# A sixth tile pair of an up projection formed from seven products, and what stands behind it in the order

## The chip, the core and the metric

The kernel runs on one core of one Trainium2 chip. The metric is the device time of one execution in microseconds (us). Five engines work side by side and meet only through semaphores: PE (matmuls), DVE and ACT (elementwise work), POOL (here mostly DMAs that add) and SP (plain DMAs). Each runs its own list of instructions in the order in which the program holds them.

## The reference

One layer of a decoder over 512 prompt rows and 8 sequences of 4 sample rows, 544 rows in all. The change lies in its last part, the convolutional feed-forward block:

```python
def _conv_ffn(h, prev, w_up, conv_w, conv_b, w_down):
    u = h @ w_up                                   # 1024 -> 8192
    u, conv_state = _causal_dwconv(u, prev, conv_w, conv_b)
    val, gate = jnp.split(u, 2, axis=-1)
    return (jax.nn.gelu(gate, approximate=True) * val) @ w_down, conv_state   # 4096 -> 1024
```

All matrix products are made in float32 accuracy from pairs of rounded high and low parts.

## The kernel before, in words

Each factor is split into a high part H and a low part L, and a product of blocks is the sum high times high, high times low, low times high: three matmuls for each of the 128-row pieces of the contraction. The up projection is made in 32 pairs p: column tile p of the value half and column tile 32+p of the gate half, 128 columns each. The normed rows lie in two halves of 272 (`b11`, `b21` for rows 0 to 271, upper and lower half of the contraction; `b12`, `b22` for rows 272 to 543).

A pair is made in one of two ways. The plain way takes eight half products of 12 matmuls each (two tiles, two halves of the contraction, two row halves; bank names `pq`). The other, from pair `PLAIN` on, forms seven products of 12 matmuls from sums of weights and sums of rows (function `pair`; banks `pux`, `puy`, `puz` and sometimes `puw`): `a11`, `a12`, `p2`, `p3`, `p1`, `p4`, `a22`. The rows' sums `t1` to `t4` are made once, ahead of the first such pair. The weights' sums are made per pair by `sums`: DVE forms p3 = s + g and g = g + g', and two adding DMAs of POOL form the rest in place, in a third loaded weight tile (`raw_up_..._s`). Banks are read in between: `e1` is bank x after `a11`, and `p2` adds onto that bank only when the copy is taken; `u4` is bank x after `p1`; from it DVE forms the gate's second row half out of bank y (`u` from `puy` and `u4`), and only then may `a22` add onto bank y.

After a pair come, per tile, the state copies, a convolution of three taps (`tap`: ACT, then DVE twice, into `uc`), and `glu`: a gelu on ACT, the product `z` on DVE, its high part `fH` on ACT and its low part `fL` on DVE. These feed the down projection, made per group of four pairs (quarter products `dn`, q = 0 to 6: one output tile c, one row half a, 12 matmuls, banks `pmdn`); the last group (pairs 28 to 31, weights `dl`) comes at the end with products of its own.

Every weight tile is rounded on ACT (`wh_...`, line 1485) and its remainder taken on DVE (`wl_...`). The order of the work is a list, `plan`, written ahead. After each step of the list (a product), the elementwise work that is due and the splits of the weights some steps ahead are put down; so each engine's order follows from the place of the products in the list. Half products of the down projection are put in behind certain products of a pair (`places`), as far as the group that they need is `ready`, which is counted in steps of the list:

```python
            places = [x for x in todo_ if x[2] in LAST_PLACES.get(p_, ("a12", "p3", "p1", "a22"))]
...
            ready[p_] = len(plan) + CHAIN + 3
```

What is left of them at the end of the list stands behind the last pair, except three that are held back. A pair whose `p1` is followed at once by another product of a pair is `apart`: its `p4` goes to a bank of its own (`puw`), and DVE, in place of ACT, forms the tile's second row half from it.

Of the kernel before, what the change touches and what calls it, by code (L numbers as in the profile page):

```python
# [11 lines left out]
F32 = mybir.dt.float32  # L12
# [5 lines left out]
P = 128  # L18
# [42 lines left out]
YA = (0.5, 0.5)  # L61
YB = (0.5, 0.5)
EARLY = 4
PLAIN = 6
FB = (1.0,)
LASTS = 6
HELD = 5
# [56 lines left out]
def hawk_step(ctx, tc, I, O):  # L124
# [18 lines left out]
    def S(name, dt=F32):  # L143
        return sp.tile([P, SLOT], dt, tag="s", name=name)
# [28 lines left out]
    def add(out, a, b):  # L173
        dve.tensor_tensor(out=out, in0=a, in1=b, op=ALU.add)  # L174
# [1033 lines left out]
    def part_pool(which):  # L1208

        if not parts:  # L1210
            trans.close()
            parts["e"] = ctx.enter_context(tc.tile_pool(name="parts", bufs=E_BUFS))
            parts["p"] = ctx.enter_context(tc.tile_pool(name="psums", bufs=2))
        return parts[which]
# [171 lines left out]
    for p_ in range(EARLY, 32):  # L1386
        if p_ < PLAIN:
            todo_ = [("q", j, u, a) for j in (p_, 32 + p_) for u in range(2) for a in range(2)]
# [20 lines left out]
    raws, usplit, used = {}, {}, [0, 0, 0]  # L1409
# [41 lines left out]
    def source(key):  # L1451
        if key[0] in "eq":
            return raws["up", key[1], ""][:, 4 * key[2]:4 * key[2] + 4, :]
        if key[0] == "dn":
            return raws[key]
        if key[0] == "dl":
            return raws[key[:2]][:, 4 * key[2]:4 * key[2] + 4, :]
        _, p_, nm = key
        if nm == "p3":
            return raws["p3", p_]  # L1460
        r = raws["up", 32 + p_ if nm in ("p1", "a22") else p_, "s" if nm in ("p2", "p4") else ""]
        if isinstance(r, list):
            return r[nm == "p4"]
        return r[:, 0:4, :] if nm in ("a11", "p1", "p2") else r[:, 4:8, :]

    def sums(p_, part):
        w = {nm: source(("s", p_, nm)) for nm in ("p1", "p2", "p4", "a22")}
        if part == 0:
            raws["p3", p_] = part_pool("p").tile([P, 4, P], F32, tag="p", name=f"p3_{p_}")
            add(raws["p3", p_], w["p2"], w["p1"])  # L1470
        else:
            add(w["p1"], w["p1"], w["a22"])
            pool.dma_start(out=w["p2"], in_=w["p1"], accum_op=ALU.add)
            pool.dma_start(out=w["p4"], in_=w["p2"], accum_op=ALU.add)  # L1474
# [21 lines left out]
    def ahead(n, lag=1):  # L1496

        def upto_(z, m, f):
            while used[z] < min(m, len(units)):
                f(units[used[z]])  # L1500
                used[z] += 1
        upto_(0, n + LOADS, lambda key: [load(r) for r in needs(key)])
        while used[2] < min(n, len(units)):
            m = used[2] + 1
            upto_(2, m, do_high)
            upto_(1, m - lag, do_low)
        upto_(1, n - lag, do_low)
        while sumq and sumq[0][0] <= n + 1:
            sums(*sumq.pop(0)[1:])
# [498 lines left out]
```

## Time and profile before

| | us |
|---|---|
| median of 3 runs (977.48 to 978.67) | 977.74 |
| the profiled execution's own time | 977.74 |
| its span | 976.0 |
| PE busy | 967.6 |
| DVE busy | 758.6 |
| ACT busy | 551.0 |
| POOL busy | 168.8 |

The span is the stretch from the first to the last instruction of the profile; 1.74 us lie around it. The share of busy time is a mean over stages: the feed-forward block runs from about 419 us to the end.

### The profile page before, as it was taken

The page shows a single profiled execution, that of the slowest core. Times are in us where ns is not written, and L with a number is a line of the kernel's source. Part 1 is how long each engine was busy: PE and PEld are TensorE (multiplying, and loading weights), DVE is VectorE, ACT ScalarE, POOL GpSimd, SP SyncE. Part 2 cuts the span into 40 slices and gives each one's busy share as a digit, 9 for nine tenths or more (in the row PEclk, how much of TensorE's full clock was granted, in tenths as well). Part 3 has the DMA queues.
Part 4 walks back from the last instruction along what each step waited for, and adds up shares of the span by engine and source line. Part 5 has one row for each costly group of instructions (what it writes and reads, how often), then busy time and mean ns, then how long its engine had stood idle before and what let it go on. Part 6 is the DMA issues. An engine that isn't in the chain of part 4 may idle for free.

```text
span 976.0 us, 20122 instructions
## 1 busy us (share of the span) xinstructions
PE 967.6 (99%) x7668; PEld 959.9 (98%) x7668; DVE 758.6 (78%) x1632; ACT 551.0 (56%) x1344; POOL 168.8 (17%) x288
## 2 busy tenths in 40 slices
PE   9999999999999999999999999999999999999997
PEld 8999999999999999999999999999999999999996
DVE  5777888857858555699967888787888888888875
ACT  6544443467476435556767665655555555556652
POOL 2152000003306331230011111101011101011024
PEclk9999999999999999999999999999999999999999
DMA  7875535632334547136157585858586766768612
GB/s 217 237 239 163 151 88 147 161 93 87 109 113 126 175 121 189 45 122 184 39 114 189 126 191 129 184 137 177 140 179 157 169 156 160 166 140 221 201 30 92
DMA packets 234204, 143.07 MB, mean 147 GB/s; under 512 B 25012, under 2 KB 218940, under 8 KB 234076
## 3 DMA queue, kind: packets, MB, share of 16 engines
q1 hardware_dynamic: 224300, 120.21, 43.9%
q0 software_dynamic: 9696, 19.42, 11.9%
q10 hardware_dynamic: 112, 2.17, 0.6%
q8 instruction: 60, 0.98, 0.4%
q14 instruction: 36, 0.29, 0.1%
HBM read 115.59 MB, written 15.17 MB: 134 GB/s over the span
## 4 chain that ended last, share of the span: by engine, by line
PE 97%; DVE 1%; ACT 1%; DMA 0%; issue 0%; SPq 0%; POOL 0%; ACTq 0%; POOLq 0%
PE pmin L165 20%; PE pmdn L165 19%; PE pux L1536 16%; PE puy L1536 8%; PE pq L1536 7%; PE pmout L165 5%; PE pmlo L165 5%; PE pmao L165 5%; PE puz L1536 4%; PE pg L165 1%; PE pvp L165 1%; PE psc L165 1%; PE ptok L165 1%; DMA pt<-pd 0%; PE ps_warm L165 0%; PE pm_first L165 0%
## 5 line engine op out<-in xcount | busy, mean ns | idle before, releaser
L165 PE MATMUL pmin<-hH,wh_in 128*128 128x256 f32 (+1 forms) x568 | 164.0, 291 | 0.0
L165 PE MATMUL pmin<-hL,wh_in 128*128 128x256 f32 (+1 forms) x568 | 162.5, 288 | 0.0
L165 PE MATMUL pmin<-hH,wl_in 128*128 128x256 f32 (+1 forms) x568 | 159.3, 288 | 0.0
L165 PE MATMUL pmdn<-fH,wh_dn 128*128 128x256 f32 (+1 forms) x448 | 129.3, 289 | 0.0
L165 PE MATMUL pmdn<-fH,wl_dn 128*128 128x256 f32 (+1 forms) x448 | 129.2, 288 | 0.0
L165 PE MATMUL pmdn<-fL,wh_dn 128*128 128x256 f32 (+1 forms) x448 | 129.0, 288 | 0.0
L165 PEld LDWEIGHTS pmin<-hH,wh_in 128*128 128x128 f32 x568 | 107.3, 189 | 1.2 <-issue 1.0
L165 PEld LDWEIGHTS pmin<-hL,wh_in 128*128 128x128 f32 x568 | 107.4, 189 | 0.1
L165 PEld LDWEIGHTS pmin<-hH,wl_in 128*128 128x128 f32 x568 | 104.8, 188 | 0.2 <-issue 0.2
L177 DVE SCALAR_TENSOR_TENSOR uc<-u,fv,uc 128x560 f32<-128x560 f32 x128 | 102.0, 797 | 1.7 <-ACT uc L1567 1.1
L165 PEld LDWEIGHTS pmdn<-fL,wh_dn 128*128 128x128 f32 x448 | 84.4, 188 | 0.0
L165 PEld LDWEIGHTS pmdn<-fH,wl_dn 128*128 128x128 f32 x448 | 84.4, 188 | 0.0
L165 PEld LDWEIGHTS pmdn<-fH,wh_dn 128*128 128x128 f32 x448 | 84.4, 188 | 0.0
L1664 ACT COPY u<-pux 128x272 f32<-128x272 f32 x52 | 20.1, 386 | 84.4 <-PE pux L1536 84.2
L168 DVE TENSOR_TENSOR u<-puy,u 128x240 f32<-128x240 f32 (+2 forms) x78 | 24.6, 343 | 48.8 <-PE puy L1536 32.2
L174 DVE TENSOR_TENSOR ft<-ft,pmdn 128x256 f32<-128x256 f32 (+1 forms) x104 | 45.0, 434 | 15.7 <-PE pmdn L165 15.7
L283 ACT ACTIVATE wh_in<-raw_in 128x512 fp32r<-128x512 f32 x70 | 42.2, 625 | 20.7 <-issue 11.0
L290 DVE TENSOR_TENSOR wl_in<-raw_in,wh_in 128x512 fp32r<-128x512 f32 x70 | 47.8, 694 | 1.0 <-ACT wh_in L283 1.0
L1567 ACT ACTIVATE uc<-u,fv 128x560 f32<-128x560 f32 x64 | 48.2, 755 | 0.0
L779 ACT ACTIVATE s<-s,st 128x256 f32<-128x256 f32 (+1 forms) x32 | 15.2, 475 | 53.8 <-DVE st L776 46.1
L168 DVE TENSOR_TENSOR wl_dn<-raw_dn,wh_dn 128x512 fp32r<-128x512 f32 x56 | 38.3, 685 | 3.8 <-ACT wh_dn L1485 3.8
L1474 POOL DMA_DIRECT2D raw_up_s<-raw_up_s x26 | 22.4, 861 | 95.8 <-DMA raw_up_s<-raw_up__11277 5.4
(761 smaller groups left out, 3388.5 us busy)
## 6 DMA issues: line engine op xcount, KB each, us to landing
raw_in<-in_w_in_dram SPq DMA_DIRECT2D x35, 512.0 KB
raw_dn<-in_w_down_dram SPq DMA_DIRECT2D x56, 256.0 KB
raw_up_s<-in_w_up_dram SPq DMA_DIRECT2D x25, 512.0 KB
raw_up_s<-raw_up_s POOLq DMA_DIRECT2D x26, 256.0 KB, 5.3
raw_ao<-in_w_attn_o_dram SPq DMA_DIRECT2D x8, 512.0 KB
raw_lo<-in_w_lru_o_dram SPq DMA_DIRECT2D x8, 512.0 KB
raw_out<-in_w_out_dram SPq DMA_DIRECT2D x8, 512.0 KB
pd<-pb SPq DMA_DIRECT2D x12, 256.0 KB
```

The costliest lines, as they stand in the source:

```text
L165: pe.matmul(out, l, r, start=start, stop=stop)
L168: dve.tensor_tensor(out=out, in0=a, in1=b, op=ALU.subtract)
L174: dve.tensor_tensor(out=out, in0=a, in1=b, op=ALU.add)
L177: dve.scalar_tensor_tensor(out=out, in0=a, scalar=s_, in1=b, op0=op0, op1=op1)
L283: act.activation(hl[0], raw, AF.Copy)
L290: (eng or dve).tensor_tensor(out=hl[1], in0=raw, in1=f32(hl[0]), op=ALU.subtract)
L779: act.activation(s3[:, j, :], s3[:, j, :], AF.Exp, bias=ng[:, j:j + 1], accum_out=sm[:, j:j + 1])
L1474: pool.dma_start(out=w["p4"], in_=w["p2"], accum_op=ALU.add)
L1536: pe.matmul(ps[:, :HN], w, x, start=start and k == 0 and i == 0, stop=stop and k == 3 and i == 2, skip_group_check=True)
L1567: act.activation(yt[j][:, 0:FLATU], u[:, 0:FLATU], AF.Copy, scale=fv[:, j:j + 1])
L1664: act.copy(e[nm_], z)
```

## The change

The constant `PLAIN` goes from 6 to 5, so pair 5, the sixth, is formed from seven products instead of eight. Its p3 lies in a slot of the general ring of 53 slots, in place of a tile of the small pool for such sums, which cannot be opened as long as the tiles of the norm before it are in use.

```diff
-PLAIN = 6
+PLAIN = 5
...
         if part == 0:
-            raws["p3", p_] = part_pool("p").tile([P, 4, P], F32, tag="p", name=f"p3_{p_}")
+            if p_ == PLAIN:
+                raws["p3", p_] = S(f"p3_{p_}")[:, 0:512].rearrange("p (k n) -> p k n", k=4)
+            else:
+                raws["p3", p_] = part_pool("p").tile([P, 4, P], F32, tag="p", name=f"p3_{p_}")
             add(raws["p3", p_], w["p2"], w["p1"])
```

With one step less in pair 5, readiness counted in steps comes at other places in each pair. Worked out from the list's code: before, no pair is `apart`; now pairs 8, 12, 16, 20, 24 and 28 are, where the down products of the next group, not yet ready, leave the place between `p1` and `p4` empty (and stand in a row a few steps later). Behind the last pair's `p4` stood five half products of the down projection, (6,4,0), (6,4,1), (6,5,1), (6,6,1) and (6,7,1); now the first two of them stand ahead of `p4`, and three are left. At the start of pair 5 no down product stands between `a12` and `p2`.

The order on DVE at pair 12, from the low part of its `p1` weights to the subtraction that frees bank y (`u44` from `puy_12`), before (in the names, the last number is the buffer's):

```order
L168 TENSOR_TENSOR wl_s_12_p1_8558<-raw_up_44__8255,wh_s_12_p1_8557 128x512
L174 TENSOR_TENSOR p3_13_8596<-raw_up_13_s_8489,raw_up_45__8487 128x512
L168 TENSOR_TENSOR wl_dn_1_7_8593<-raw_dn_1_7_8323,wh_dn_1_7_8592 128x512
L174 TENSOR_TENSOR raw_up_45__8487<-raw_up_45__8487 128x512
L177 SCALAR_TENSOR_TENSOR z11_8634<-uc11_8512,fv_264,uc43_8533 128x512
L177 SCALAR_TENSOR_TENSOR z11_8634<-uc11_8512,fv_264,uc43_8533 128x32
L168 TENSOR_TENSOR wl_s_12_p4_8615<-raw_up_12_s_8257,wh_s_12_p4_8614 128x512
L174 TENSOR_TENSOR ft6_7660<-ft6_7660,pmdn_1_6_1_8621 128x288
L168 TENSOR_TENSOR wl_s_12_a22_8640<-raw_up_44__8255,wh_s_12_a22_8639 128x512
L1543 MEMSET u44_8675 128x2
L168 TENSOR_TENSOR u44_8675<-puy_12_8598,u4_12_8673 128x240
L168 TENSOR_TENSOR u44_8675<-puy_12_8598,u4_12_8673 128x8x4
```

And the same place after:

```order
L168 TENSOR_TENSOR wl_s_12_p1_8607<-raw_up_44__8302,wh_s_12_p1_8606 128x512
L168 TENSOR_TENSOR wl_s_12_p4_8645<-raw_up_12_s_8304,wh_s_12_p4_8644 128x512
L177 SCALAR_TENSOR_TENSOR z11_8681<-uc11_8559,fv_264,uc43_8580 128x512
L177 SCALAR_TENSOR_TENSOR z11_8681<-uc11_8559,fv_264,uc43_8580 128x32
L168 TENSOR_TENSOR wl_s_12_a22_8665<-raw_up_44__8302,wh_s_12_a22_8664 128x512
L174 TENSOR_TENSOR ft7_7712<-ft7_7712,pmdn_1_7_1_8668 128x288
L168 TENSOR_TENSOR wl_s_13_a11_8687<-raw_up_13__8427,wh_s_13_a11_8686 128x512
L1546 MEMSET u44_8722 128x2
L168 TENSOR_TENSOR u44_8722<-puy_12_8648,u4_12_8720 128x240
L168 TENSOR_TENSOR u44_8722<-puy_12_8648,u4_12_8720 128x8x4
```

The first low part of the next pair's weights now stands ahead of the subtraction, and between `p1` and `a22` PE has one product instead of two.

The order on DVE at the end, from the second and third tap of tile 63 (`uc63`, the gate tile of pair 31) to the low part of the last pair's result (`fL31`), before:

```order
L177 SCALAR_TENSOR_TENSOR uc63_13070<-u63_13025,fv_264,uc63_13070 128x560
L168 TENSOR_TENSOR wl_dn_6_6_13074<-raw_dn_6_6_12812,wh_dn_6_6_13073 128x512
L168 TENSOR_TENSOR wl_dn_6_7_13093<-raw_dn_6_7_12854,wh_dn_6_7_13092 128x512
L174 TENSOR_TENSOR ft4_7426<-ft4_7426,pmdn_6_4_0_13113 128x256
L177 SCALAR_TENSOR_TENSOR uc31_13131<-u31_12965,fv_264,uc31_13131 128x560 x2
L177 SCALAR_TENSOR_TENSOR z31_13149<-uc31_13131,fv_264,uc63_13070 128x512
L177 SCALAR_TENSOR_TENSOR z31_13149<-uc31_13131,fv_264,uc63_13070 128x32
L168 TENSOR_TENSOR wl_dl_0_0_13153<-raw_dl_0_12877,wh_dl_0_0_13152 128x512
L168 TENSOR_TENSOR wl_dl_1_0_13156<-raw_dl_1_12902,wh_dl_1_0_13155 128x512
L174 TENSOR_TENSOR ft4_7426<-ft4_7426,pmdn_6_4_1_13133 128x288
L168 TENSOR_TENSOR fL31_13178<-z31_13149,fH31_13177 128x544
```

The same stretch on DVE after, from the second low part of the last group's weights on (ahead of it stand `wl_dn_6_6`, `wl_dn_6_7`, the addition to `ft4`, the last tap of `uc63` and `wl_dl_0_0`):

```order
L168 TENSOR_TENSOR wl_dl_1_0_13163<-raw_dl_1_12929,wh_dl_1_0_13162 128x512
L168 TENSOR_TENSOR wl_dl_2_0_13168<-raw_dl_2_12954,wh_dl_2_0_13167 128x512
L168 TENSOR_TENSOR wl_dl_3_0_13192<-raw_dl_3_12977,wh_dl_3_0_13191 128x512
L174 TENSOR_TENSOR ft5_7471<-ft5_7471,pmdn_6_5_1_13171 128x288
L177 SCALAR_TENSOR_TENSOR uc31_13189<-u31_13015,fv_264,uc31_13189 128x560 x2
L177 SCALAR_TENSOR_TENSOR z31_13214<-uc31_13189,fv_264,uc63_13136 128x512
L177 SCALAR_TENSOR_TENSOR z31_13214<-uc31_13189,fv_264,uc63_13136 128x32
L168 TENSOR_TENSOR wl_dl_0_1_13195<-raw_dl_0_12906,wh_dl_0_1_13194 128x512
L168 TENSOR_TENSOR wl_dl_1_1_13218<-raw_dl_1_12929,wh_dl_1_1_13217 128x512
L1756 STREAM_TRANSPOSE ffn_rows_s3_13225<-sfT_5298 128x256
L174 TENSOR_TENSOR ft6_7581<-ft6_7581,pmdn_6_6_1_13198 128x288
L168 TENSOR_TENSOR fL31_13242<-z31_13214,fH31_13241 128x544
```

Four low parts of the last group's weights now stand ahead of the taps of `uc31`, where none stood, and two more and a transposition between `z31` and `fL31`.

The order on ACT over the same stretch, from the gelu of tile 63 to the last tile's high part `fH31`, before (`u31` from `pux_31` is the copy of the last product `p4`):

```order
L1578 ACTIVATE uc63_13070<-uc63_13070,fv_264 128x560
L1485 ACTIVATE wh_dn_6_7_13092<-raw_dn_6_7_12854 128x512
L1681 COPY u31_12965<-pux_31_12908 128x240
L1681 COPY u31_12965<-pux_31_12908 128x8x4
L1559 COPY u31_12965<-sfT_5298 128x8x2
L1560 COPY sfT_5298<-u31_12965 128x16
L1561 COPY stage_p_5299<-u31_12965 128x2
L1567 ACTIVATE uc31_13131<-u31_12965,fv_264 128x560
L1485 ACTIVATE wh_dl_0_0_13152<-raw_dl_0_12877 128x512
L1485 ACTIVATE wh_dl_1_0_13155<-raw_dl_1_12902 128x512
L1485 ACTIVATE wh_dl_2_0_13159<-raw_dl_2_12925 128x512
L1586 ACTIVATE fH31_13177<-z31_13149 128x544
```

And after (the row ahead of these is again the gelu of tile 63, the row behind them one more split, and then `fH31`):

```order
L1488 ACTIVATE wh_dl_1_0_13162<-raw_dl_1_12929 128x512
L1488 ACTIVATE wh_dl_2_0_13167<-raw_dl_2_12954 128x512
L1684 COPY u31_13015<-pux_31_12960 128x240
L1684 COPY u31_13015<-pux_31_12960 128x8x4
L1562 COPY u31_13015<-sfT_5298 128x8x2
L1563 COPY sfT_5298<-u31_13015 128x16
L1564 COPY stage_p_5299<-u31_13015 128x2
L1570 ACTIVATE uc31_13189<-u31_13015,fv_264 128x560
L1488 ACTIVATE wh_dl_3_0_13191<-raw_dl_3_12977 128x512
L1488 ACTIVATE wh_dl_0_1_13194<-raw_dl_0_12906 128x512
L1488 ACTIVATE wh_dl_1_1_13217<-raw_dl_1_12929 128x512
```

Two splits instead of one stand between the gelu and the copies of `p4`, and the split `wh_dl_3_0`, for which `wl_dl_3_0` on DVE waits, stands behind the first tap of `uc31`.

## The prediction

> **What bounds the kernel now.** I read the page first (busy time by engine, then the shares of the chain that ended last), then PE's waits, then the stages that the change touches.
>
> ```profile
> span 976.0 us, 20122 instructions
> PE 967.6 (99%) x7668; PEld 959.9 (98%) x7668; DVE 758.6 (78%) x1632; ACT 551.0 (56%) x1344; POOL 168.8 (17%) x288
> PE 97%; DVE 1%; ACT 1%; DMA 0%; issue 0%; SPq 0%; POOL 0%; ACTq 0%; POOLq 0%
> ```
>
> PE is busy 99% of the span and carries 97% of the chain. The list of what PE waited for (us in total, times, longest) has three entries, two of which are:
>
> ```profile
> PE pst L909 <- DVE ss L787: 0.7, 1, 0.7
> PE pm_first L165 <- DVE wh_in L285: 0.6, 1, 0.6
> ```
>
> None lies in the feed-forward block. So the time is PE's work, every product removed counts in full, and every new wait of PE is added in full. The question is only whether removing a product makes waits where there were none. Durations below come from the profiled execution, whose own time is the median of the runs, 977.74; 1.74 of it lie around the span and are taken as unchanged.
>
> **The saved product.** The chain of waits around pair 8 (start, duration, engine, tile, instructions):
>
> ```profile
> 542.72 1.50 PE pux L1536 x12
> 544.22 1.41 PE pmdn L165 x12
> 545.63 1.51 PE pux L1536 x12
> 547.14 1.51 PE puy L1536 x12
> ```
>
> These are `p1`, a half product of the down projection, `p4` and `a22`. A product costs 1.51. Pair 5 needs seven, not eight: **-1.5**. That is 0.15% of the time; a measurement of this kernel can tell some 0.2% (2.0 us) from no change. So with no new wait the change would not be seen at all, and the waits decide.
>
> **The tail.** The chain of waits at the end of the last pair:
>
> ```profile
> 921.91 1.60 PE pmdn L165 x12
> 923.51 1.52 PE pux L1536 x12
> 925.03 8.88 PE pmdn L165 x68
> 933.91 0.04 issue
> 933.95 1.00 PE pmdn L165 x4
> ```
>
> The last `p4` ends at 925.03. Five half products (1.60 each, the row of 921.91) fill PE until 933.0, and of the next product nine matmuls come before the last tile's rows are read. What must be made meanwhile stands on ACT and DVE; first ACT's timeline (start, duration, line, out<-in, idle before):
>
> ```profile
> 925.74 0.77 ACT L1578 ACTIVATE uc<-uc,fv 128x560 f32<-128x560 f32 x1 [2.03 <-DVE uc L177]
> 926.41 0.62 ACT L1485 ACTIVATE wh_dn<-raw_dn 128x512 fp32r<-128x512 f32 x1
> 926.93 0.42 ACT L1681 COPY u<-pux 128x240 f32<-128x240 f32 x2
> ...
> 927.70 0.76 ACT L1567 ACTIVATE uc<-u,fv 128x560 f32<-128x560 f32 x1
> 928.37 1.66 ACT L1485 ACTIVATE wh_dl<-raw_dl 128x512 fp32r<-128x512 f32 x3
> 931.12 0.66 ACT L1586 ACTIVATE fH<-z 128x544 fp32r<-128x544 f32 x1 [1.09 <-DVE z L177]
> ```
>
> And DVE's:
>
> ```profile
> 923.94 0.69 DVE L168 TENSOR_TENSOR wl_dn<-raw_dn,wh_dn 128x512 fp32r<-128x512 f32 x1
> 924.55 0.45 DVE L174 TENSOR_TENSOR ft<-ft,pmdn 128x288 f32<-128x288 f32 x1
> 924.91 0.80 DVE L177 SCALAR_TENSOR_TENSOR uc<-u,fv,uc 128x560 f32<-128x560 f32 x1
> ...
> 928.49 1.64 DVE L177 SCALAR_TENSOR_TENSOR uc<-u,fv,uc 128x560 f32<-128x560 f32 x2 [0.41 <-ACT uc L1567]
> 930.17 0.91 DVE L177 SCALAR_TENSOR_TENSOR z<-uc,fv,uc 128x512 f32<-128x512 f32 x2
> 931.00 1.29 DVE L168 TENSOR_TENSOR wl_dl<-raw_dl,wh_dl 128x512 fp32r<-128x512 f32 x2
> ...
> 932.57 0.72 DVE L168 TENSOR_TENSOR fL<-z,fH 128x544 fp32r<-128x544 f32 x1
> ...
> 935.98 0.44 DVE L1753 STREAM_TRANSPOSE ffn_rows_s<-sfT 128x256 f32<-128x256 f32 x1
> ```
>
> The reader is to see the chain `p4` copy 926.93, first tap 927.70, two taps to 930.17, `z` to 931.00, `fH` to 931.78, `fL` to 933.29, while PE reads these rows at about 934.2 (933.0 and nine matmuls, a ninth of 1.60 over twelve each being 0.13). So the cover is about 1 us. Around 933.9 PE lost something to other work: four matmuls of 0.13 took 1.00 with the issue gap 0.04, where 0.53 is their due; of the 0.5 between, some 0.2 may be the last matmul's length, so I take 0.3 as lost.
>
> After, three half products stand behind `p4`, so with `p4` again ending at 925.03 PE is at 925.03 + 3 x 1.60 + 1.20 = 931.03 when it asks for `fH31`. The chain, on the other hand, gets longer, by steps read off the rows. A low part costs DVE 0.61 (923.94 to 924.55), an addition 0.36 (924.55 to 924.91), a high part costs ACT 0.52 (926.41 to 926.93).
>
> - One more low part ahead of the last tap of `uc63`: +0.61. One more high part on ACT behind the gelu: +0.52. The copies of `p4` come at 926.93 + 1.13 = 928.06, the first tap 0.77 later, at 928.83, and ends at 929.59.
> - `wl_dl_3_0` on DVE needs `wh_dl_3_0`, which ACT makes right behind that tap: 928.83 + 0.67 + 0.62 = 930.12. Then 0.61 for the low part and 0.36 for the addition to `ft5`: the taps of `uc31` begin at 931.09, not at 928.49. What is queued behind the waiting low part is the whole rest of the chain.
> - Taps 1.68, so `z` at 932.77 and `fH31` 0.95 later, from 933.72 to 934.38. PE waits 934.38 - 931.03 = 3.35.
> - DVE is through with `z` at 933.60; two low parts (1.22), the transposition (0.36 to the next start) and an addition (0.36) stand ahead of `fL31`, which then ends at 935.54 + 0.72 = 936.26. PE has two matmuls (0.27) between `fH31` and this: it waits 936.26 - 934.38 - 0.27 = 1.61.
>
> Together 4.96, less the 0.3 already lost: **+4.7**. Bounds: if nothing on the chain got longer, 933.29 against 931.03 + 0.27, less 0.3, leaves +1.7; if `wh_dl_3_0` came behind two further high parts, +4.7 + 1.04 = +5.7. I take the chain as worked out, since each step is an order fixed on in-order engines.
>
> **The six pairs with `p4` right behind `p1`.** The timelines of the three engines in pair 8:
>
> ```profile
> 546.97 0.29 PE L1536 MATMUL puy<-t4H,wh_s_a 128*128 128x272 f32 x1
> ```
>
> ```profile
> 544.25 0.39 ACT L1664 COPY u<-pux 128x272 f32<-128x272 f32 x1 [0.57 <-PE pux L1536]
> ```
>
> ```profile
> 544.67 0.51 DVE L168 TENSOR_TENSOR u<-puy,u 128x240 f32<-128x240 f32 x2 [1.44 <-ACT u L1664]
> ```
>
> `u4` is copied as soon as `p1` ends, DVE subtracts until 545.18, and `a22` asks for bank y at 546.97: 1.79 of cover. Without the half product between (1.41) the cover is 0.38. A low part (0.61) that stands ahead of the subtraction uses it up and costs 0.23; one more high part on ACT (0.62) ahead of the copy makes it 0.85; two low parts and an addition on DVE give 0.61 + 0.61 + 0.45 - 0.38 = 1.29. Nothing lost is the lower end, 6 x 1.29 = 7.7 the upper. The order after has one low part ahead in pair 12, and DVE was idle 1.44 before the subtraction in pair 8, so I go near the one-instruction price, 0.4 a pair: **+2.4**. The half product itself isn't lost: it stands elsewhere in the list.
>
> **The start of pair 5.** `p2` adds onto bank x only when ACT has copied `e1`. In the order after, the copy stands behind the high parts of the row sums `t4H`, the copy of `u36`'s first rows, a split, its other copies with the states, and one more split; and no down product stands between `a12` and `p2`. In the timeline of ACT these were:
>
> ```profile
> 481.67 1.19 ACT L1308 ACTIVATE t4H<-h2f 128x544 fp32r<-128x544 f32 x2
> 482.76 0.36 ACT L1627 COPY u<-pq 128x272 f32<-128x272 f32 x1
> 483.02 0.63 ACT L1485 ACTIVATE wh_dn<-raw_dn 128x512 fp32r<-128x512 f32 x1
> ```
>
> 1.19 + 0.36 + 0.63 + 0.77 (copies and states, 926.93 to 927.70) + 0.62 + the copy 0.39 = 3.96. If ACT begins this when pair 4 ends, it is through 3.96 - 2 x 1.51 = 0.94 after `a12`: **+0.9**. If all of it is still there when `a11` ends, 2.45; if ACT was ahead, 0. I take the middle case.
>
> **What is costed at nothing.** Pair 5 now has seven splits, not four (3 x 0.61 more on DVE, 3 x 0.62 on ACT), two sums on DVE (0.61 each, taken as a low part of the same size) and two adding DMAs with a third loaded tile. The stretches around it (length, then PE, PEld, DVE, ACT, POOL busy) and the DMA's issue to landing:
>
> ```profile
> 480.00:490.00 10.00, 10.00 (x82) 10.00 (x81) 9.71 (x18) 6.94 (x18) 0.94 (x1) 1.00 0.41 114
> 490.00:500.00 10.00, 10.00 (x82) 10.00 (x81) 5.50 (x10) 6.01 (x21) 0.87 (x1) 1.00 0.62 150
> ```
>
> ```profile
> raw_up_s<-raw_up_s POOLq DMA_DIRECT2D x26, 256.0 KB, 5.3
> ```
>
> DVE's 3.05 fit into the 4.5 idle of the second stretch, not into the 0.29 of the first; without that cover 1.5 to 3 would show in pair 5's products. PE waited for no such DMA; if one came a whole landing late, 5.3. SP's loads shift by one tile, with the DMA engines at 0.41 to 0.62. I take 0 for all of it.
>
> **Sum:** -1.5 + 4.7 + 2.4 + 0.9 = +6.5, so 977.7 + 6.5 = **984.2 us**.
>
> **A rule on the clock.** At PE's start, in its timeline:
>
> ```profile
> 1.00 2.50 PE L165 MATMUL ps_warm<-ones 128*128 128x128 f32 x10 [1.00 <-POOL ones L219]
> ...
> 6.69 0.39 PE L165 MATMUL ps_warm<-ones 128*128 128x128 f32 x2
> ```
>
> The same matmul takes 0.25 in the first row and 0.20 in the second: a slow start of some 5.7 us, and between then and the tail no wait of PE is above 0.7. The Trainium skill, page "TensorE: Matmul & The Clock Gate", Part 1, section "What's actually happening", has PE fall to half its clock after an idle window of about 3.4 us and come back after as long a busy one; no run here shows PE idle for so long. By that page, as an estimate, the tail's wait would cost 1.7 more (half of 3.4), 985.9 in all; without it the sum stands.
>
> **Rivals.**
> 1. The tail alone: the six pairs and pair 5's start are hidden. -1.5 + 4.7 = +3.2: 981.0. For it speaks the idle DVE before the subtraction (1.44); against it a cover of only 0.38.
> 2. The six pairs pay in full: -1.5 + 4.7 + 7.7 + 0.9 = +11.8: 989.5. For it speaks a DVE busy 78% on the mean; against it the same idle.
> 3. PE slows after the tail's wait of 3.35 (at half rate for as long as the slow start, 5.7, half of it lost): +6.5 + 2.9 = +9.4: 987.1. The rows of the start speak for a clock that has to be earned, the small ratio of 0.25 to 0.20 against the full price.
> 4. Not slower: DVE and ACT run ahead, so that the four low parts in the tail are done while they would idle (2.03 on ACT before the gelu, 0.41 on DVE before the taps). Then the tail costs its lower bound and the rest is hidden: -1.5 + 1.7 = +0.2, 977.9. It decides where all new waits together stay under 3.5. Against it: `wl_dl_3_0` cannot start ahead of `wh_dl_3_0`, which stands behind the first tap.
> 5. No new wait at all: 977.7 - 1.5 = 976.2. Against it: 925.03 + 4.8 lies ahead of even the old `fH31`.
>
> **How the numbers follow.** The forecast, with its terms somewhat off (+4.5 to +8.5), has 0.53; rival 1 0.18, 2 0.07, 3 0.09, 4 0.08, 5 0.05. The time is that of the likeliest, 984.2. The range runs from 980.3 (the tail alone, its term 0.7 smaller) to 988.0 (the clock's loss, with a margin of 0.9): it leaves out rivals 2, 4 and 5, 0.20. Faster by over 0.2% needs 975.8 or less: 0.02, the lower edge of rival 5. Same: the rest of 5 and rival 4 and the lowest edge of rival 1, 0.13. Slower: 0.85.
>
> **What would show it.** PE's list of waits should have entries where it had none: the down products of the last group waiting for `fH31` (about 3.4) and `fL31` (about 1.6), `a22` of pairs 8 to 28 in steps of four for DVE's subtraction (0.2 to 0.9 each), and `p2` of pair 5 for ACT's copy (about 0.9). PE's busy time should fall by 1.5. If the wait for `fH31` is under 1, the tail's step is wrong; if PE waits for the adding DMAs of pair 5, what I costed at nothing is; if matmuls behind the tail's wait take longer than 0.13, the clock is.

## The result and the profile after

| | before | after |
|---|---|---|
| median, us | 977.74 | 987.54 (985.97 to 988.15, 5 runs) |
| ratio to before | | 1.0096 (95% interval 1.0085 to 1.0108) |
| the profiled execution's own time | 977.74 | 986.73 |
| its span | 976.0 | 984.9 |

The changed kernel is slower by 9.8 us in the median and 9.0 in the profiled execution, which is the one taken apart below. The page of the changed kernel, its first lines and the shares of the chain that ended last:

```profile
span 984.9 us, 20143 instructions
PE 968.4 (98%) x7656; PEld 960.0 (97%) x7656; DVE 765.8 (78%) x1653; ACT 551.5 (56%) x1334; POOL 169.2 (17%) x290
PE 87%; DVE 6%; ACT 3%; DMA 2%; issue 1%; SPq 0%; DVEq 0%; ACTq 0%
```

Twelve matmuls are gone, yet PE's busy time rose by 0.8 where 1.5 less was due: some of the others got slower. And DVE and ACT now carry a share of the chain (followed back from a wait, the chain runs over other engines for longer than PE stood still, so its shares are not losses). The list of PE's waits (us in total, times, longest), as far as they lie in the feed-forward block:

```profile
PE pmdn L165 <- ACT fH L1589: 3.4, 1, 3.4
PE pmdn L165 <- DVE fL L168: 1.4, 1, 1.4
PE puy L1539 <- DVE u L168: 1.3, 2, 1.1
...
PE pux L1539 <- ACT e L1667: 1.0, 1, 1.0
```

All four are where the prediction had put them. At the kernel's start two waits differ as well (`pm_first` 1.1, not 0.6, and a new one of 0.5 on the DMA of the input rows), but the matmuls behind them start at 9.20, and at 9.22 before: they cost nothing. The chain that makes the last tile's rows, on ACT and on DVE (the timelines; the product behind the last `p4` starts at 929.35, at 925.03 before):

```profile
932.55 0.42 ACT L1684 COPY u<-pux 128x240 f32<-128x240 f32 x2
...
933.31 0.76 ACT L1570 ACTIVATE uc<-u,fv 128x560 f32<-128x560 f32 x1
933.98 2.17 ACT L1488 ACTIVATE wh_dl<-raw_dl 128x512 fp32r<-128x512 f32 x4
938.22 0.66 ACT L1589 ACTIVATE fH<-z 128x544 fp32r<-128x544 f32 x1 [2.06 <-DVE z L177]
```

```profile
934.62 0.69 DVE L168 TENSOR_TENSOR wl_dl<-raw_dl,wh_dl 128x512 fp32r<-128x512 f32 x1 [1.18 <-ACT wh_dl L1488]
935.24 0.45 DVE L174 TENSOR_TENSOR ft<-ft,pmdn 128x288 f32<-128x288 f32 x1
935.60 1.63 DVE L177 SCALAR_TENSOR_TENSOR uc<-u,fv,uc 128x560 f32<-128x560 f32 x2
937.27 0.92 DVE L177 SCALAR_TENSOR_TENSOR z<-uc,fv,uc 128x512 f32<-128x512 f32 x2
938.10 1.29 DVE L168 TENSOR_TENSOR wl_dl<-raw_dl,wh_dl 128x512 fp32r<-128x512 f32 x2
...
940.00 0.70 DVE L168 TENSOR_TENSOR fL<-z,fH 128x544 fp32r<-128x544 f32 x1
```

DVE stands idle 1.18 for `wh_dl`, with the taps of `uc31` queued behind the waiting low part. PE's timeline at the same place (start, duration, line, form, wait and what ended it):

```profile
935.20 0.29 PE L165 MATMUL pmdn<-fH,wl_dl 128*128 128x288 f32 x1
938.92 0.40 PE L165 MATMUL pmdn<-fH,wh_dl 128*128 128x288 f32 x1 [3.44 <-ACT fH L1589]
940.76 0.61 PE L165 MATMUL pmdn<-fL,wh_dl 128*128 128x288 f32 x1 [1.44 <-DVE fL L168]
...
942.50 0.44 PE L165 MATMUL pmdn<-fL,wh_dl 128*128 128x288 f32 x1
942.74 0.44 PE L165 MATMUL pmdn<-fH,wl_dl 128*128 128x288 f32 x1
...
946.63 0.29 PE L165 MATMUL pmdn<-fH,wh_dl 128*128 128x288 f32 x1
946.77 0.29 PE L165 MATMUL pmdn<-fL,wh_dl 128*128 128x288 f32 x1
```

The reader is to see the starts: 942.50 to 942.74 is 0.24 from matmul to matmul, 946.63 to 946.77 is 0.14, the usual step. Between the wait and 946.5 PE is never idle and yet runs at half its pace. The windows say why; the third column from the end is the granted clock (us, then busy time and instructions of PE, PEld, DVE, ACT, POOL, clock, DMA share, GB/s). Of the kernel before, 5.75 us at the same place in the work, and of the changed one, the stretch behind the wait and the one after it:

```profile
934.50:940.25 5.75, 5.75 (x45) 5.70 (x45) 4.79 (x13) 1.85 (x4) 3.53 (x7) 1.00 0.37 115
```

```profile
940.75:946.50 5.75, 5.74 (x25) 5.71 (x26) 2.55 (x7) 1.20 (x3) 5.24 (x10) 0.50 0.39 107
946.75:948.00 1.25, 1.25 (x12) 1.25 (x11) 0.46 (x1) 0.41 (x2) 0.70 (x2) 1.00 0.05 7
```

In quarter microseconds the granted clock turns to 0.50 at 939.7 and back at 946.5: 6.8 us. Of these, PE worked in 5.75, and made 25 matmuls where before it made 45: 20 x 0.13 = 2.6 us lost.

The sum for the profiled execution, with waits taken from start to start, which is 0.1 to 0.3 more than the list's: -1.5 (a product), +1.15 (`p2` of pair 5), +1.24 and +0.41 (`a22` of pairs 20 and 24), +3.59 and +1.70 (`fH31`, `fL31`), less the 0.3 that was lost there before, +2.6 (half clock) = +8.9. The spans differ by 8.9. Matched matmul by matmul from the end, the two traces agree with this: the distance between them grows from 1.5 to 6.4 over the tail's two waits and from 6.4 to 9.0 over the slow matmuls.

### The profile page after: what moved, and what is told of

Its sections match the earlier page's. It is cut to its first block, busy times and chain, and to the rows that moved or that the text cites. A ratio compares the mean times of both kernels' runs of the same rounds, so it can differ in the third digit from the quotient of the medians.

```text
span 984.9 us, 20143 instructions
## 1 busy us (share of the span) xinstructions
PE 968.4 (98%) x7656; PEld 960.0 (97%) x7656; DVE 765.8 (78%) x1653; ACT 551.5 (56%) x1334; POOL 169.2 (17%) x290
## 3 DMA queue, kind: packets, MB, share of 16 engines
q10 hardware_dynamic: 112, 2.17, 0.6%
## 4 chain that ended last, share of the span: by engine, by line
PE 87%; DVE 6%; ACT 3%; DMA 2%; issue 1%; SPq 0%; DVEq 0%; ACTq 0%
PE pmin L165 20%; PE pmdn L165 17%; PE pux L1539 14%; PE puy L1539 8%; PE pmout L165 5%; PE pmlo L165 5%; PE pmao L165 5%; PE puz L1539 4%; PE pq L1539 3%; DMA raw_up_s<-in_w_up_dram 1%; DVE uc L177 1%; PE pg L165 1%; PE pvp L165 1%; PE psc L165 1%; PE ptok L165 1%
## 5 line engine op out<-in xcount | busy, mean ns | idle before, releaser
L1581 ACT ACTIVATE uc<-uc,fv 128x560 f32<-128x560 f32 x32 | 24.5, 766 | 24.9 <-DVE uc L177 23.3
```

The costliest lines, as they stand in the source:

```text
L1581: act.activation(yg[:, 0:FLATU], yg[:, 0:FLATU], AF.Gelu_apprx_tanh, bias=fv[:, 224 + p_:225 + p_])
```

## The experiments

Theory A: the loss comes from the places of the down products in the list (the tail's two waits, then the clock, two of the six pairs, the start of pair 5). Theory B: pair 5's own additional splits, sums and DMAs cost it. A second question was whether the slow matmuls come from PE's idle time or from something that runs beside them.

**Only the product, with the list as before.** The edit to the changed kernel:

```diff
-LAST_PLACES = {29: ('p3', 'p1', 'a22'), ...
+LAST_PLACES = {5: ('p1', 'a22'), 29: ('p3', 'p1', 'a22'), ...
```

> Pair 5 keeps its seven products, but may take half products of the down projection only behind p1 and a22, two and not four. From pair 6 on the list is then that of before: no pair has p4 right behind p1, and five half products stand behind the last p4. Theory A (the loss is the places of the down products: tail 3.4 + 1.4, slow PE after it about 3, pair 20 and 24 about 1.3, start of pair 5 about 1.0): only the start of pair 5 is left, -1.5 + 1.0 = -0.5, 977.2 us, no PE wait for fH, one of about 1.0 for e. Theory B (the seven products of pair 5 cost it, by their splits, sums and adding DMAs): 982 or more, with PE waits spread over pairs 5 to 10.

Measured: 977.84, ratio 1.0001 (0.9992 to 1.0010). Its waits:

```profile
PE pux L1539 <- ACT e L1667: 1.0, 1, 1.0
```

This is the only new one, 1.15 from start to start; 977.7 - 1.5 + 1.15 would be 977.4, and the 0.4 between lies within the spread. 9.7 us are gone with one entry of a table, while pair 5 does all its seven products. Theory B falls.

**Only the tail, with six plain pairs.** The edit to the kernel before:

```diff
-LAST_PLACES = {29: ('p3', 'p1', 'a22'), 30: ('p3', 'p1', 'a22'), 31: ('p1', 'a22')}
+LAST_PLACES = {31: ('p1', 'a22')}
```

> The kernel before (six plain pairs) with pairs 29 and 30 taking four half products each, not three; so three and not five stand behind the last p4, and nothing else moves. Theory A: PE waits 3.4 for fH and 1.4 for fL, then its clock is at half for some 6 us, about 3 lost: +7.6, 985.3 us, without any change to pair 5. Theory A without the clock (the slow matmuls behind the wait have another cause): +4.6, 982.3. Theory B: 977.7, since pair 5 is as before.

Measured: 984.38, ratio 1.0066 (1.0054 to 1.0078). Its waits and its windows:

```profile
PE pmdn L165 <- ACT fH L1586: 3.4, 1, 3.4
PE pmdn L165 <- DVE fL L168: 1.2, 1, 1.2
```

```profile
936.75:943.50 6.75, 4.91 (x19) 4.57 (x20) 4.54 (x11) 2.00 (x4) 4.65 (x9) 0.50 0.33 101
946.75:948.00 1.25, 1.25 (x12) 1.25 (x11) 0.91 (x2) 0.12 (x1) 0.00 (x0) 1.00 0.00 0
```

Nothing of pair 5 is changed here, and 6.6 of the 9.8 us are there: 5.0 of waits (3.57 and 1.71 from start to start, less 0.3) and the rest of clock: 1.6 by the medians, 1.8 in the profiled execution (984.50 against 977.74). The clock was low for as long as in the changed kernel, 6.75, but PE stood still for 1.8 of it, which is why it cost less than the 3 that I had expected.

**Filling the wait.** Repeated matmuls, overwritten by the real product, ahead of the first product behind the held list, in the changed kernel (24, 12 and 18) and in the one above (24). They come ahead of the wait and lengthen nothing as long as they are shorter than it.

```diff
         for k in range(CH):
...
+            if (q, c, a, k) == (QL, 0, 1, 0):
+                for _ in range(24):
+                    pe.matmul(ps[:, :hi - lo], wh, xh, start=True, stop=False, skip_group_check=True)
             mm(ps[:, :hi - lo], wh, xh, k == 0, False)
```

> The changed kernel with 24 more matmuls (a repeat of the first one of the first product after the held list, overwritten by it) put ahead of that product, where PE would soon wait: 24 x 0.13 = 3.2 us of work in a wait of 3.4. If the slow matmuls from 940 to 946 come from PE's idle time, they are gone: the wait for fH is about 0.3, that for fL stays at 1.4, the granted clock stays at 1.00, and the time falls by about 3 to 984.5. If they come from something else that runs there (DMAs, the reads of the last weights), they stay and the time stays at 987.5. If filling itself costs, the time rises by up to 3.2.

> before_three_left (six plain pairs, three half products behind the last p4; 984.4, clock at half for 6.8 us) with 24 repeated matmuls in the wait for fH. If the clock falls for PE's idle time, it stays at 1.00 here too and the time falls by the loss at half clock, 2 to 3: 981.4 to 982.4; the wait for fL stays at 1.2. If the wait alone makes the loss, 984.4.

Measured: 984.35 in the changed kernel (987.54 without), 982.45 in the other (984.38 without). The changed kernel with 24, its waits and the stretch at the place where the clock was 0.50:

```profile
PE pmdn L165 <- DVE fL L168: 1.4, 1, 1.4
...
PE pmdn L165 <- ACT fH L1589: 0.2, 1, 0.2
```

```profile
940.75:946.50 5.75, 5.49 (x42) 5.49 (x43) 3.72 (x10) 2.33 (x5) 5.38 (x11) 1.00 0.40 119
```

POOL's work runs beside it as before (5.38 us busy, 5.24 without the filling), and the clock stays at 1.00; PE makes 42 matmuls in the 5.75 us, not 25. `fL31` is as late as before. So what vanishes is the clock's loss, and the clock fell for PE's idle time: work that nobody needs made the kernel faster. By the medians it is 3.2 us; between the two profiled executions it is 2.4, and the filled one waits 0.4 more at `a22` of the pairs, which leaves some 2.8, near the 2.6 counted above. In the other kernel the gain was 1.9, and 1.8 had been put down to the clock in its profiled execution.

> The changed kernel with 12 repeated matmuls ahead of the first product behind the held list (24 in changed_fill_24): PE's idle time for fH is then about 1.9, followed by one matmul and 1.4 for fL. If the clock falls only after an idle time of 3 or more, it stays at 1.00 and the time is that of 24, 984.4. If shorter idle times add up over such a stretch, the clock falls as without the filling and the time is 987.5.

> The changed kernel with 18 repeated matmuls in the wait for fH: idle times of about 1.1 and 1.4 with one matmul between. With 24 (0.2 and 1.4) the clock stayed up, with 12 (1.8 and 1.4) it fell in most executions, some 1.3 us lost in the median. If what counts is the idle share of a stretch of some us, the time lies between, 984.4 to 985.6, and the clock stays up in most executions; if any idle time of over 1 is enough, 985.6 or more.

Measured: 985.64 with 12 (984.32 to 987.47) and 985.45 with 18 (984.40 to 985.71). The profiled execution with 12:

```profile
PE pmdn L165 <- ACT fH L1589: 1.8, 1, 1.8
...
PE pmdn L165 <- DVE fL L168: 1.4, 1, 1.4
```

```profile
941.25:944.50 3.25, 3.25 (x16) 3.25 (x15) 1.61 (x6) 1.03 (x2) 2.87 (x7) 0.50 0.42 127
```

The clock fell here too, though no wait is longer than 1.8: from 941.1 to 944.5, 3.4 us. With 18 (waits of 1.0 and 1.4, one matmul between) it fell in the profiled execution from 941.4 to 944.8. Both of my conditions were too simple. It isn't one idle time of 3 us that counts, and neither of the two expectations for 12 came out: the loss was about 1.3, between none and all. With 18 the time lay in the range expected for the idle share, but the clock did not stay up in most executions: the mean granted clock was 0.997 in three of five and 0.999 in two (the kernel before has 0.998 to 1.000, its clock falling only behind PE's last matmuls). Not all of the spread is clock: of the two at 0.999 one took 984.40 and the other 985.21.

The traces of these runs, read in stretches of 3.41 us, show what does count. Three of the stretches, the changed kernel, then with 18, then with 24 (the windows again, PE's busy time behind the length):

```profile
936.26:939.67 3.41, 0.40 (x1) 0.19 (x1) 3.34 (x8) 1.18 (x2) 0.00 (x0) 1.00 0.00 0
```

```profile
937.97:941.38 3.41, 0.95 (x5) 0.74 (x6) 3.41 (x10) 1.18 (x2) 1.27 (x3) 1.00 0.24 90
```

```profile
937.13:940.55 3.42, 2.21 (x15) 1.77 (x13) 3.38 (x8) 1.18 (x2) 0.26 (x1) 1.00 0.00 0
```

The clock fell at the end of the first and of the second, at 939.67 and 941.38, and not at the end of the third. Why the stretches are cut there, and what the other traces show, stands in the last section.

**Fewer splits ahead of the last taps.** The edit to `before_three_left`:

```diff
-LASTS = 6
+LASTS = 3
```

> before_three_left (six plain pairs, three half products behind the last p4) with the last steps' splits put later (LASTS 3, not 6): fewer low parts of the last group's weights stand ahead of the taps of uc31 on DVE. If the tail's loss is the chain that got longer plus the clock, as I worked out, most of it goes: the cover that is short alone costs 1.7 to 3.1, in several waits under 1.5, the clock stays at 1.00, and the time is 979.5 to 980.9, against 984.4. If the loss is the cover alone (three products, not five), the time stays at 984.4.

Measured: 981.32 (980.52 to 982.96), ratio 1.0034 (1.0021 to 1.0046). The waits of the profiled execution, itself 980.52:

```profile
PE pmdn L165 <- DVE wl_dl L168: 1.4, 2, 1.2
...
PE pmdn L165 <- DVE fL L168: 0.8, 1, 0.8
```

The long chain is gone with the splits, and 3.1 of 6.6 us with it. What is left, 2.2 in three waits and some clock in the slower executions (mean granted clock 0.999 at 980.52, 0.996 at 982.96), is the short cover of three products: DVE must do those splits somewhere. The median lies 0.4 above the range, for that clock.

**Pairs with `p4` right behind `p1`.** The changed kernel with five left at the end, and the same with the states' transposition one pair earlier:

```diff
-LAST_PLACES = {29: ('p3', 'p1', 'a22'), ...
+LAST_PLACES = {25: ('p1', 'a22'), 29: ('p3', 'p1', 'a22'), ...
```

```diff
-        for g0, g1, p_ in ((0, 2, 19), (2, 3, 27)):
+        for g0, g1, p_ in ((0, 2, 18), (2, 3, 27)):
```

> The changed kernel with pair 25 taking two half products, not four: five half products stand behind the last p4 as before, and pairs 8, 12, 16, 20 and 24 keep p4 right behind p1. Theory A: -1.5 + 1.0 (start of pair 5) + 1.2 (pair 20) + 0.4 (pair 24) = +1.1, 978.8 us, no wait for fH. My forecast's price for such pairs (0.4 each, five of them) gives +1.5, 979.2. Theory B: 982 or more.

> apart_five_left (five half products at the end, pairs 8 to 24 in steps of four with p4 right behind p1) with the transposition and output of the first half of the sample states moved from behind pair 19 to behind pair 18. If a22 of pair 20 waited 1.2 because this transposition (0.7 on DVE) stood ahead of the subtraction there, that wait is gone and the time is 979.5 - 1.2 = 978.3. If a pair with p4 right behind p1 waits by itself, as my forecast priced it, pair 20 still waits 0.4 to 1.2 and the time stays within 0.5 of 979.5.

Measured: 979.50, ratio 1.0018 (1.0009 to 1.0026), and 979.68, ratio 1.0015 (1.0006 to 1.0024). With five products left at the end, 8.0 of the 9.8 us are gone, and no wait for `fH31` or `fL31` is in the list: that is the tail's two waits and the clock. Its profiled execution, 978.92, is near the 978.8 of theory A; the median is 0.7 above. PE's timeline at `a22` of pair 20, in the first and in the second:

```profile
747.92 0.36 PE L1539 MATMUL puy<-t4H,wh_s_a 128*128 128x272 f32 x1 [1.06 <-DVE u L168]
```

```profile
748.70 0.36 PE L1539 MATMUL puy<-t4H,wh_s_a 128*128 128x272 f32 x1 [0.49 <-DVE u L168]
```

What stood ahead of the subtraction on DVE in the first (its timeline there):

```profile
744.28 0.70 DVE L1756 STREAM_TRANSPOSE ffn_rows_s<-sfT 128x512 f32<-128x512 f32 x1
744.91 0.87 DVE L177 SCALAR_TENSOR_TENSOR z<-uc,fv,uc 128x512 f32<-128x512 f32 x2
745.70 0.69 DVE L168 TENSOR_TENSOR wl_s_a<-raw_up__10160,wh_s_a 128x512 fp32r<-128x512 f32 x1
746.30 0.44 DVE L174 TENSOR_TENSOR ft<-ft,pmdn 128x288 f32<-128x288 f32 x1
746.66 0.68 DVE L168 TENSOR_TENSOR wl_s_a<-raw_up__10285,wh_s_a 128x512 fp32r<-128x512 f32 x1
747.28 0.40 DVE L168 TENSOR_TENSOR u<-puy,u 128x240 f32<-128x240 f32 x1
```

Of five pairs only 20 and 24 wait in this execution. Moving the 0.70 of the transposition shortens the wait in pair 20 by 0.57 (1.06 to 0.49) and not by all of it: the row without a gap behind it (`z`, two low parts, an addition) is late by itself. Both theories of that run were half right, and 0.6 us can't be seen in its time, whose interval is as wide.

**The slot.** The kernel before with the p3 of its first such pair in a slot of the general ring:

```diff
-            raws["p3", p_] = part_pool("p").tile([P, 4, P], F32, tag="p", name=f"p3_{p_}")
+            if p_ == PLAIN:
+                raws["p3", p_] = S(f"p3_{p_}")[:, 0:512].rearrange("p (k n) -> p k n", k=4)
+            else:
+                raws["p3", p_] = part_pool("p").tile([P, 4, P], F32, tag="p", name=f"p3_{p_}")
```

> The kernel before with only the second part of the change: the p3 of its first pair of this kind (pair 6) in a slot of the general ring instead of the small pool. If the slot costs nothing, as I assumed: 977.8, within 0.2%. If it takes a buffer that the ring needs, loads or elementwise results behind it wait for their slot and PE has new waits: 979 or more.

Measured: 978.23, ratio 1.0004 (0.9996 to 1.0013). No new wait above 0.2: the slot costs nothing that can be told.

**A version that beats both.** The first experiment and one number more, which puts the rounding of the row sums two steps later, so that `t4H` comes behind the copy `e1` on ACT:

```diff
-TX = 4
+TX = 6
```

> Pair 5 by seven products with half products only behind its p1 and a22, as in p5_two_places, and the rounding of the row sums t3, t1 and t4 put two steps later (TX 6, not 4), so that ACT's t4H no longer stands ahead of the copy e1. Theory A (only the wait for e1, 1.15, was left): no wait of PE at the start of pair 5, -1.5, 976.2 us. If that wait was cover for something else that is late (t4 for a22, p3's weights), it comes back under another name and the time stays at 977.8. By the theory that the seven products of pair 5 cost their own work elsewhere: no change from 977.8.

Measured: 976.56 (976.04 to 977.49), ratio 0.9985 (0.9977 to 0.9994): a small gain, but outside the spread. Its page and ACT's timeline, where the reader is to see `t4H` two microseconds behind `e`:

```profile
span 973.9 us, 20121 instructions
```

```profile
484.28 0.36 ACT L1667 COPY e<-pux 128x272 f32<-128x272 f32 x1
...
486.25 1.20 ACT L1308 ACTIVATE t4H<-h2f 128x544 fp32r<-128x544 f32 x2
```

The three waits of PE that are left in the list are those of the kernel before. The gain of 1.4 in the median is the product's 1.5 us; its interval reaches from 0.6 to 2.2.

## Why the prediction came out as it did, point by point

- **The saved product** (-1.5) is right: with the waits away the gain is 1.4 to 1.5 (0.9985 of 978.0). PE's busy time did not fall by 1.5 but rose by 0.8, because of the slow matmuls.
- **The tail's chain** (+4.7) is right, in its mechanism and its size: 3.44 and 1.44 of wait against 3.35 and 1.61. In the trace after, set back by the 4.3 by which `p4` ends later, the steps stand about 0.2 later than worked out: copies of `p4` 932.55 (928.06 + 4.3), taps of `uc31` 935.60 (931.09), `z` 937.27 (932.77). One reading was wrong in it: the sum counted two matmuls (0.27) between the two waits, and there is one, at 938.92, which makes the second wait 0.13 longer. That the order was to be read as a chain with the earlier durations is shown by this, and that the splits lengthen it by the run with LASTS 3.
- **The start of pair 5** (+0.9): 1.0 in the list, 1.15 from start to start, from ACT's copy `e1`, as said; moving `t4H` removed it.
- **The six pairs** (+2.4) were taken too dear, and the shape was wrong: 0.4 for each of six was forecast, two pairs paid 1.24 and 0.41 and the other four nothing (with 24 repeats, whose list is the same there, pair 28 paid some 0.4 as well). A mean price is not what a train of instructions costs; the wait is decided by what else DVE has in hand at that pair.
- **What was costed at nothing** cost nothing: no wait on a DMA in the feed-forward block, none on pair 5's splits, none for the slot.
- **The clock** was left out of the sum, and that is the step that failed. It stood as a rival of chance 0.09 with the price 2.9; measured were 2.6 in the profiled execution, and 3.2 in the median by the filled kernel. I had held the ratio of 0.25 to 0.20 at the start against the full price. That ratio was misread: a merged row's time holds the whole length of its last matmul, 0.28 to 0.42, so a row of two can't be divided by two. Eight `ps_ta` matmuls from start to start show the ratio; the row from before, and two rows of the changed kernel:

```profile
5.07 1.78 PE L473 MATMUL ps_ta<-ident,x 128*128 128x128 f32 x8
```

```profile
4.77 1.04 PE L473 MATMUL ps_ta<-ident,x 128*128 128x128 f32 x8
5.64 0.39 PE L165 MATMUL ps_warm<-ones 128*128 128x128 f32 x2
```

  They take 5.07 to 6.69, 0.20 each, before, and 4.77 to 5.64, 0.11 each, after. The trace's records of the clock begin at 6.58 in the first and at 4.42 in the second, both with 1.00 (ahead of its first record a window shows 1.00 too, for want of one), and the steps change from 0.21 to 0.11 right there. So PE starts at about half rate, and the start spoke for the full price.

  The trace of before also held the fall itself, though I wrote that no run showed PE idle for so long: PE's last matmul ends at 969.94, and the clock is at 0.50 from 972.55 to the end of the span.

  That the price came so near is luck in part: 5.7 was the length of the slow start, and the half clock here lasted 6.8, in which PE worked for 5.75. The price itself is in the rows behind the wait, 0.24 against 0.14. The Trainium skill, page "TensorE: Matmul & The Clock Gate", Part 1, section "What's actually happening", gave half the clock after an idle window of about 3.4 us, in windows that run freely; here the clock fell to 0.50 behind waits of 3.4 and 1.4, for 6.8 us, and behind 1.8 and 1.4 for 3.4. The halving and the windows agree, and the traces show that such a window need not be idle throughout: PE worked up to 0.95 us in it.
- So +6.5 forecast and +9.8 measured, with the forecast's own terms at 6.3 (8.9 less 2.6), the clock 2.6 (both in the profiled execution, which is 9.0 slower), and the remaining 0.8 of the median spread between executions.
- **The range** held because the clock's loss had been taken into it: its upper end was that rival with a margin of 0.9, and the 987.54 lies above the rival's 987.1, within the margin. The forecast's own 984.2, which had the chance of 0.53, was 3.3 short. Of the rivals on the other side, none had room: the total of new waits was 7 us.

## What to carry to other kernels

Where PE is busy all the time, the cost of an edit is not its instructions but where it leaves the ones it did not touch; before a product is removed, write the chains of the other engines at the places where the order moved and count what is left to cover them. A wait of PE of some microseconds has to be charged with the slow clock behind it as well, here half as much again as the wait. And when the order is counted in steps, give the freed places back (one entry in a table) before judging the edit.

## What the runs showed of the hardware that I had not expected

The granted clock fell to 0.50 with no single wait above 1.0 to 1.8 us when two stood close together (1.8 and 1.4 with one matmul between; 1.0 and 1.4 in the profiled execution of the run with 18), for 3.4 us; behind 3.4 and 1.4 it lasted 6.8, twice as long. With 0.2 and 1.4 it stayed at 1.00 in the profiled execution.

The traces show what this depends on. The clock's changes lie on a grid of 3.413 us: in the changed kernel at 4.42, 939.67, 946.50 and 984.05, which are 274, 2 and 11 times 3.413 apart, and with 12 at 5.88, 941.13, 944.54 and 982.09 (274, 1 and 11). The grid lies otherwise in each execution (first record from 4.4 to 7.4). What PE worked in the stretch between two points of the grid decided at its end:

| trace | stretch | PE busy, us of 3.41 | clock behind it |
|---|---|---|---|
| after | 936.26 to 939.67 | 0.40 | 0.50 |
| before_three_left | 933.27 to 936.68 | 0.68 | 0.50 |
| changed_fill_12 | 937.72 to 941.13 | 0.76 | 0.50 |
| before (its end) | 969.14 to 972.55 | 0.80 | 0.50 |
| changed_fill_18 | 937.97 to 941.38 | 0.95 | 0.50 |
| p5_two_places (its end) | 968.47 to 971.88 | 1.73 | 1.00 |
| before_three_fill_24 | 937.82 to 941.24 | 2.14 | 1.00 |
| three_left_lasts3 | 932.45 to 935.86 | 2.17 | 1.00 |
| changed_fill_24 | 937.13 to 940.55 | 2.21 | 1.00 |
| after (pair 20's wait) | 745.11 to 748.53 | 2.34 | 1.00 |

So in these traces it fell for up to 0.95 and not for 1.73 or more; where between them the limit lies, no run shows. It came back at the end of the first stretch that PE filled (3.41): after one with 12 and 18, after two in the changed kernel and in `before_three_left`, where PE still waited for `fL31` in the first (2.33 and 1.51 busy). That gives the 3.4 and the 6.8.

Where the grid happens to lie then decides whether two short waits share a stretch, which fits that executions of one kernel differed by 1 to 2 us: `before_three_fill_24` took 982.4 three times at a mean granted clock of 0.999, and 984.3 and 984.4 at 0.997. The executions that were not profiled have no trace, so for them this is argued. And 24 matmuls without use in a wait saved 3.2 us in the median.
